# Units of modulation in the opening of a hybrid block kernel: nine of 1, 2, 2, 2, 2, 2, 2, 2 and 1 k tiles in place of eight of two

## The chip, the core and the metric

The kernel runs on one core of one Trainium2 chip. The metric is device time in microseconds. Several executions were timed; the tables give their median. One further execution was profiled, and everything that is said of single instructions comes from it.

The core's engines work side by side and meet through semaphores: TensorE (PE, with its weight loads as PEld), VectorE (DVE), ScalarE (ACT), GpSimd (POOL) and SyncE (SP), which in this kernel issues most of the DMAs. Sixteen DMA engines move the data between HBM and the on-chip memory.

## What is computed

One block with two branches, on 256 tokens of x and 256 tokens of a context, both of width 2048, in f32. Only the start of it matters here:

```python
mod = jax.nn.silu(c) @ w_ada[l] + b_ada[l]
shift, scale, gate = jnp.split(mod[:, None, :], 3, axis=-1)
...
xn = rmsnorm(h, norm_gain[l]) * (1.0 + scale) + shift
cn = rmsnorm(hc, norm_gain[l]) * (1.0 + scale_c) + shift_c
aq, ak, av, ag, hq, hff, hfb, hi, hg, ma, mb = split_columns(xn @ w_in[l])
```

`w_ada` is 2048 x 6144, `w_in` is 2048 x 19456. Columns 0 to 4095 of `mod` (shift and scale) are needed before any normalized column is complete, and each projection sums over all 2048 columns of `xn`. After that come an attention over a window and the context, a gated linear recurrence (HGRN2) in both directions, two output projections, a merge and a last projection.

## The kernel before

**Precision.** A projection operand is split into a high part (`wh`, `xH`), rounded to float32r, and a low part (`wl`, `xL`), the remainder. Three products, high by high, low by high and high by low, are summed in PSUM, so one product of f32 matrices takes three matmuls.

**The opening** (lines 239 to 501) loads x and the context into `X`, transposes them on TensorE (`turn_x`, line 282) so that the model dimension lies on the partitions, and computes the rows' reciprocal roots (`spread_rs`). The 2048 columns are 16 *k tiles* of 128 (`KT` = 16). The list `UNITS` (line 451) cuts them into units `(k, n)`: the first k tile and how many.

For each unit three things happen:

- **Modulation** (`modulation(k, n)`, line 311, a generator). It computes shift and scale for the unit's n x 128 columns, for c and for the context's c at once. In four steps (`k0` = 0, 4, 8, 12) SP loads the unit's columns of `w_ada`, four row tiles at a time, in two DMAs (shift and scale, line 321), into a buffer `raw` of a ring of four; TensorE multiplies them (line 323), four row tiles in four column groups of the array, into the bank `pa`. The bank is copied to `part` (lines 330 and 332), transposed (`tq`, line 336) and reduced on DVE to the columns `mod` (lines 339 to 345). A buffer of the ring always has room for two k tiles, whatever n is.
- **Normalizing** (`modulate(kt)`, line 352), for each k tile of the unit: DVE makes `xm` (line 360), ACT adds the shift and rounds it to `xH` (line 361), DVE takes the remainder `xL` (line 367).
- **First projections** (`first_pieces`, line 407). The opening projects onto 768 columns of `w_in` on the way: 512 of one forget gate and 256 of the other, loaded per unit by `first_loads` (line 389; two DMAs, line 66) and split on ACT and DVE by `first_highs` (lines 400 and 404). Each k tile has 18 matmuls of 512 moving columns (lines 421 and 427), in four pieces of 4, 4, 4 and 6, into six PSUM banks that are held through the whole opening.

**The order** is written out by hand for PE, SP, ACT and DVE (line 460). The first unit's modulation runs first, with fill matmuls into an unused bank in between (`rest`, line 445). Then, for each unit u, its operands are split and normalized, and its pieces run with the modulation of unit u + 1 pushed in between: `plan` (line 476) puts two steps behind piece 0, the other two and the copy to `part` behind piece 2, and the transposes `tq` behind piece 3. Behind piece 3 SP also issues the `w_in` loads of unit u + 1. In a unit of two k tiles the pieces 4 to 7 of its second k tile follow `tq`; they are what TensorE does while DVE and ACT normalize the next unit. SP takes its DMAs in this order, and a load of `w_ada` waits until TensorE has read the ring's buffer four steps before.

After the last unit the six banks are turned to forget gates (`forget`, line 216), and the ordinary projections begin with `proj_tok` (line 745; line 100 is the first of their matmuls). From there only TensorE's order is written out; the order on the other engines comes from priorities and a planner that simulates the engines' times.

Of the kernel before, what the change touches and what calls it, by code (L numbers as in the profile page):

```python
# [17 lines left out]
KT = D // P  # L18
# [20 lines left out]
def block_kernel(ctx: ExitStack, tc: tile.TileContext, x, c, cx, c_ctx, w_ada, b_ada, norm_gain, w_in,  # L39
# [199 lines left out]
    with pl("st", reuse_waits="tile") as st:  # L239
# [65 lines left out]
        def spread_rs():  # L305
            pr_ = ps.tile([P, 512], F32, tag="al2", name="prs")
            pe.matmul(pr_, ones, dgx, start=True, stop=True)
            with tc.high_priority(2 * PRIO):
                act.activation(rsb, pr_, AF.Copy)
# [79 lines left out]
        def first_loads(u, k, n):  # L389

            raws[u] = [wload(w_in, k * P, n, (co,), nc_)[0][:, : n * nc_] for co, nc_ in ((C_FF, 512), (C_FB, 256))]

        def first_highs(u, n):

            tg, nb = FIRST[u % 3]
            f = [wp.tile([P, 1024], F32R, tag=tg_, name=tg_, bufs=3)[:, : n * 512] for tg_ in ("wh", "wl")]
            qt = fp.tile([P, 2, 512], F32R, tag=tg, name="wq", bufs=nb)
            q = [qt[:, r, : n * 256] for r in range(2)]
            for hl, raw in zip((f, q), raws[u]):
                act.activation(hl[0], raw, AF.Copy)  # L400
            fv = [a.rearrange("p (k c) -> p k c", k=n) for a in f]
            chunks[u] = [[a[:, :, :256] for a in fv], [a.rearrange("p (k c) -> p k c", k=n) for a in q],
                         [a[:, :, 256:] for a in fv]]
            return [lambda hl=hl, raw=raw: dve.tensor_tensor(hl[1], raw, hl[0].bitcast(F32), op=ALU.subtract)
                    for hl, raw in zip((f, q), raws[u])]
# [35 lines left out]
        def take(g, n):  # L441
            for _ in range(n):
                next(g, None)
# [4 lines left out]
            for q in range(n):  # L448
                pe.transpose(idle[:, (q % 4) * P: (q % 4 + 1) * P], ident, ident)

        UNITS = [(k, 2) for k in range(0, KT, 2)]
        with tc.manual_schedule(engines={mybir.EngineType.PE, mybir.EngineType.SP}):
            for i in range(4):
                turn_x(i)
# [5 lines left out]
        with tc.manual_schedule(engines={mybir.EngineType.PE, mybir.EngineType.SP, mybir.EngineType.Activation,  # L460
                                         mybir.EngineType.DVE}):
            unit = modulation(*UNITS[0])
            for i in range(4):
                rest(8)
                take(unit, 1)
                if i == 1:
                    spread_rs()
            first_loads(0, *UNITS[0])
            take(unit, 1)
# [6 lines left out]
            plan = {0: 2, 2: 3, 3: 9}  # L476
            for u, (k, n) in enumerate(UNITS):
                lows = first_highs(u, n)
# [3 lines left out]
                after = iter(())  # L482
                if u + 1 < len(UNITS):
                    after = modulation(*UNITS[u + 1])
                if u == 3:
                    bounds()
                for i, _ in enumerate(first_pieces(first, u, k, n)):
                    take(after, plan.get(i, 0))
                    if i == 3 and u + 1 < len(UNITS):
                        first_loads(u + 1, *UNITS[u + 1])  # L490
# [1074 lines left out]
```

## Time and profile before

| | us |
|---|---|
| median of 3 runs | 1593.74 |
| lowest, highest | 1592.25, 1598.02 |
| the profiled execution | 1593.52 |
| its span, from first to last instruction | 1591.7 |
| PE busy in the span | 1567.9 |
| DVE busy | 1182.9 |
| ACT busy | 855.4 |

The profiled execution took 1.8 us more than its span, which is what lies around it. Its time is 0.22 us below the median of the three runs. Busy time counts an engine's instructions; matmuls overlap in the array, and their ends are modelled, so a busy TensorE isn't TensorE at its peak. What counts for it are starts: from one start to the next is what a matmul really takes. Times in the trace are counted from the start of the span. In a row of the timeline stand start, length, engine, line, what is written from what, the tile's form and how many instructions are merged; in brackets the idle time before it and what ended it. A load's "us to landing" runs from its issue on the queue to its completion.

### The profile page before, as it was taken

The numbers are of one execution on the slowest core, as the hardware profiler recorded it, in microseconds if no ns is written. First come the engines' busy times: TensorE is split into PE (matmuls) and PEld (weight loads), VectorE is DVE, ScalarE is ACT, GpSimd is POOL, SyncE is SP. The second block draws the span as 40 slices with busy tenths as digits, with TensorE's granted clock in tenths as the row PEclk, the third lists the DMA queues.
The fourth block names the chain that finished last, engine by engine and source line by source line (L and its number), as shares of the span: only waits on it lengthen the run. The fifth ranks groups of instructions, "written<-read, shape, count | busy, mean of one in ns | idle before, by whom it ended". The sixth has DMA issues, their size and how long they took to land. (4 is left out here: it accounts for less than half of the span.)

```text
span 1591.7 us, 27553 instructions
## 1 busy us (share of the span) xinstructions
PE 1567.9 (99%) x10810; PEld 1341.4 (84%) x10810; DVE 1182.9 (74%) x1745; ACT 855.4 (54%) x1338; POOL 140.5 (9%) x280
## 2 busy tenths in 40 slices
PE   7999999999999999999999999999999999999998
PEld 4567899999888888888888888888887888888887
DVE  4449677777888887787978888887976677757764
ACT  4334443333555555655665566666565776744442
POOL 2000000000000000111121212121112000000000
PEclk9999999999999999999999999999999999999999
DMA  9995533434444444777778777787778854458761
GB/s 369 386 387 174 166 110 131 134 131 133 146 133 136 136 135 130 243 234 230 245 264 271 256 259 244 238 271 240 234 262 262 261 165 149 158 175 288 238 196 70
DMA packets 240851, 333.81 MB, mean 210 GB/s; under 512 B 12080, under 2 KB 157904, under 8 KB 239952
## 3 DMA queue, kind: packets, MB, share of 16 engines
q1 hardware_dynamic: 212048, 249.54, 48.1%
q0 software_dynamic: 19168, 64.08, 11.9%
q10 hardware_dynamic: 9504, 18.42, 3.2%
q8 instruction: 85, 1.39, 0.4%
q14 instruction: 46, 0.38, 0.1%
HBM read 300.53 MB, written 31.47 MB: 209 GB/s over the span
## 5 line engine op out<-in xcount | busy, mean ns | idle before, releaser
L85 ACT ACTIVATE wh<-raw 128x1024 fp32r<-128x1024 f32 x292 | 307.5, 1060 | 257.3 <-PE pj L101 179.1
L86 DVE TENSOR_TENSOR wl<-raw,wh 128x1024 fp32r<-128x1024 f32 x292 | 354.4, 1219 | 122.1 <-ACT wh L85 116.2
L100 PE MATMUL pj<-wh,xHL 128*128 128x512 f32 (+1 forms) x832 | 325.0, 392 | 0.7 <-ACT sg L219 0.7
L101 PE MATMUL pj<-wh,xHL 128*128 128x512 f32 (+1 forms) x832 | 320.3, 386 | 0.0
L103 PE MATMUL pj<-wl,xHL 128*128 128x512 f32 (+1 forms) x832 | 218.5, 386 | 0.0
L100 PEld LDWEIGHTS pj<-wh,xHL 128*128 128x128 f32 x832 | 156.9, 189 | 32.7 <-ACT sg L219 1.9
L101 PEld LDWEIGHTS pj<-wh,xHL 128*128 128x128 f32 x832 | 156.9, 189 | 29.9
L103 PEld LDWEIGHTS pj<-wl,xHL 128*128 128x128 f32 x832 | 154.0, 188 | 31.4
L635 ACT ACTIVATE wh<-T 128x1024 fp32r<-128x1024 f32 x69 | 73.2, 1061 | 149.6 <-DVE T L616 74.0
L635 ACT ACTIVATE wh<-raw 128x1024 fp32r<-128x1024 f32 x92 | 96.9, 1054 | 63.7 <-PE pj L734 23.4
L154 PE MATMUL pj<-xHL,wh 128*128 128x512 f32 x512 | 130.3, 395 | 0.6 <-DVE sgm L1073 0.5
L636 DVE TENSOR_TENSOR wl<-raw,wh 128x1024 fp32r<-128x1024 f32 x92 | 112.0, 1218 | 9.2 <-ACT wh L635 9.1
L154 PEld LDWEIGHTS pj<-xHL,wh 128*128 128x128 f32 x512 | 92.4, 189 | 18.0 <-DVE sgm L1073 0.9
L636 DVE TENSOR_TENSOR wl<-T,wh 128x1024 fp32r<-128x1024 f32 x69 | 84.2, 1220 | 29.7 <-ACT wh L635 29.7
L157 PEld LDWEIGHTS pj<-xHL,wl 128*128 128x128 f32 x512 | 69.9, 190 | 5.8 <-issue 0.7
L157 PE MATMUL pj<-xHL,wl 128*128 128x256 f32 x512 | 71.5, 282 | 0.6 <-issue 0.6
L204 DVE SCALAR_TENSOR_TENSOR acc<-hgw,cg,acc 128x512 f32<-128x512 f32 x60 | 44.8, 747 | 32.7 <-DMA hgw<-in_w_ada_dram 32.7
L918 DVE TENSOR_TENSOR A<-A,X 128x512 f32<-128x512 f32 x96 | 61.7, 684 | 1.6 <-ACT Kmt L848 0.7
L541 POOL DMA_DIRECT2D hgw<-in_w_ada_dram x64 | 34.8, 544 | 273.9 <-DVE acc L204 211.0
L660 PE MATMUL pm<-S,wh 128*128 128x512 f32 x224 | 56.8, 395 | 0.5 <-ACT s L667 0.5
L616 DVE TENSOR_TENSOR T<-raw,T 128x1024 f32<-128x1024 f32 x46 | 56.0, 1218 | 0.0
L616 DVE TENSOR_TENSOR raw<-raw 128x1024 f32<-128x1024 f32 x23 | 28.2, 1225 | 34.9 <-DMA raw<-in_w_in_dram 34.9
(356 smaller groups left out, 3017.9 us busy)
## 6 DMA issues: line engine op xcount, KB each, us to landing
raw<-in_w_in_dram SPq DMA_DIRECT2D x300, 512.0 KB, 4.5
raw<-in_w_ada_dram SPq DMA_DIRECT2D x64, 512.0 KB, 8.0
hgw<-in_w_ada_dram POOLq DMA_DIRECT2D x64, 256.0 KB, 4.4
raw<-in_w_o_hgrn_dram SPq DMA_DIRECT2D x32, 512.0 KB, 3.8
raw<-in_w_o_attn_dram SPq DMA_DIRECT2D x32, 512.0 KB, 4.2
raw<-in_w_out_dram SPq DMA_DIRECT2D x28, 512.0 KB, 3.6
F<-F POOLq DMA_DIRECT2D x16, 512.0 KB, 6.8
F<-F ACTq DMA_DIRECT2D x13, 512.0 KB, 4.4
```

Of the source, the lines that this page charges most:

```text
L85: last_hi[0] = act.activation(h[:, :n], raw[:, :n], AF.Copy).ins
L86: last_lo[0] = dve.tensor_tensor(lo[:, :n], raw[:, :n], h[:, :n].bitcast(F32), op=ALU.subtract).ins
L100: pe.matmul(o, s[0], m[0], start=first, stop=False)
L101: pe.matmul(o, s[1], m[0], start=False, stop=False)
L103: pe.matmul(o, s[0], m[1], start=False, stop=last)
L154: pe.matmul(o.rearrange("p (a t) -> p a t", a=2), h[:, j, cs_], xHL[:, :, k0 + j, :T], start=k0 + j == 0, stop=False)
L157: pe.matmul(o[:, :T], lo[:, j, cs_], xH[:, k0 + j, :T], start=False, stop=k0 + j == KT - 1)
L616: dve.tensor_tensor(o, x_, y_, op=ALU.subtract)
L635: act.activation(h, src, AF.Copy)
L636: dve.tensor_tensor(lo, src, h.bitcast(F32), op=ALU.subtract)
L660: pe.matmul(m_[z].rearrange("p (z a t) -> p z a t", z=2, a=2), h[:, k, :], mv(k), start=fresh and k == 0, stop=False, skip_group_check=True)
L918: dve.tensor_tensor(av, av, f.unsqueeze(3).to_broadcast([P, 2, n2, b]), op=ALU.mult)
```

## The change

One line. `UNITS` was eight units of two k tiles, (0, 2), (2, 2) to (14, 2). Now it is nine: (0, 1), then (1, 2), (3, 2) to (13, 2), then (15, 1).

```diff
-        UNITS = [(k, 2) for k in range(0, KT, 2)]
+        UNITS = [(0, 1)] + [(k, 2) for k in range(1, KT - 1, 2)] + [(KT - 1, 1)]
```

All that takes `(k, n)` follows. With n = 1 a modulation step loads two times 256 KB in rows of 512 B where n = 2 loads two times 512 KB in rows of 1 KB, its matmuls have 256 moving columns instead of 512, `tq` has two transposes instead of four, the unit's `w_in` loads are 256 and 128 KB, and the unit has the pieces 0 to 3 only. `plan` stays as it is, so in unit 0 the transposes of unit 1 stand behind its last piece. The step's buffers and the ring of four stay the same. The code that runs `bounds` with unit 3 now does so one k tile earlier.

## The prediction

> **What bounds the kernel now.** I read the page first, for the stage that the change touches, then the opening in stretches, then the instructions of TensorE and of the DMA queue in it.
>
> ```profile
> span 1591.7 us, 27553 instructions
> PE 1567.9 (99%) x10810; PEld 1341.4 (84%) x10810; DVE 1182.9 (74%) x1745; ACT 855.4 (54%) x1338; POOL 140.5 (9%) x280
> ...
> PE   7999999999999999999999999999999999999998
> ...
> DMA  9995533434444444777778777787778854458761
> ...
> raw<-in_w_ada_dram SPq DMA_DIRECT2D x64, 512.0 KB, 8.0
> raw<-in_w_in_dram SPq DMA_DIRECT2D x300, 512.0 KB, 4.5
> ```
>
> A slice is 39.8 us. TensorE is full from the second slice to the last, so what moves the end of the opening moves the end of the kernel about one to one. The DMA engines are full only in the first three slices. The next view gives stretches of the opening; the columns are PE, PEld, DVE, ACT and POOL busy, then granted clock, DMA share and GB/s.
>
> ```profile
> 0.00:10.00 10.00, 3.57 (x17) 3.57 (x18) 2.76 (x8) 4.07 (x9) 4.30 (x15) 1.00 0.81 309
> 10.00:20.00 10.00, 7.25 (x53) 6.34 (x52) 9.24 (x31) 8.26 (x19) 3.39 (x8) 1.00 1.05 392
> 33.00:40.00 7.00, 5.65 (x39) 2.22 (x41) 2.96 (x7) 0.91 (x2) 0.00 (x0) 1.00 1.08 388
> 86.80:99.60 12.80, 12.80 (x73) 7.81 (x72) 5.61 (x13) 3.85 (x9) 0.00 (x0) 1.00 1.09 386
> 118.20:124.30 6.10, 6.10 (x33) 5.01 (x30) 4.09 (x9) 3.92 (x6) 0.00 (x0) 1.00 0.64 229
> ```
>
> The DMA stream runs at its full 386 to 392 GB/s from 10 us until the last w_ada load, at some 118 us. TensorE is full as well. Its instructions in order of time (start, length) show which of the two is ahead; the last row groups all modulation matmuls to 170 us (busy, mean ns, idle before them):
>
> ```profile
> 20.78 1.06 PE L323 MATMUL pa<-raw,acc 128*32 128x512 f32 x8
> 21.77 1.09 PE L449 MATMUL idle<-cs 128*128 128x128 f32 x8
> 28.74 0.66 PE L449 MATMUL idle<-cs 128*128 128x128 f32 x4
> 32.35 0.73 PE L427 MATMUL pj<-xHL,wh 128*128 128x512 f32 x2
> 37.42 1.07 PE L323 MATMUL pa<-raw,acc 128*32 128x512 f32 x8
> 39.84 1.07 PE L323 MATMUL pa<-raw,acc 128*32 128x512 f32 x8 [1.35 <-DMA raw<-in_w_ada_dram]
> 42.34 0.60 PE L336 MATMUL tq<-cs,part 128*128 128x128 f32 x4
> 42.69 0.71 PE L427 MATMUL pj<-xHL,wh 128*128 128x512 f32 x2
> 46.89 0.62 PE L427 MATMUL pj<-xHL,wh 128*128 128x512 f32 x2
> 51.81 2.03 PE L323 MATMUL pa<-raw,acc 128*32 128x512 f32 x16
> 124.29 0.62 PE L427 MATMUL pj<-xHL,wh 128*128 128x512 f32 x2
> 132.59 0.50 PE L100 MATMUL pj<-wh,xHL 128*128 128x512 f32 x1
> L323 PE MATMUL pa<-raw,acc 128*32 128x512 f32 x256 | 31.8, 601 | 1.4 <-DMA raw<-in_w_ada_dram 1.4
> ```
>
> Call the time from one unit's first projection to the next one's a phase: it holds the unit's 36 projections and the four modulation steps of the unit behind it. Unit 0 starts at 32.35, unit 1 at 46.89, unit 7 at 124.29, and the opening ends at 132.59. Units 1 to 6 take 77.40 us, 12.90 each. A unit's loads are 4.19 MB of w_ada (8 of 512 KB) and 0.79 MB of w_in (512 and 256 KB), 12.87 us at 387 GB/s. So **both are at their limit at once**: the last step of unit 1 waits 1.35 us for its load at 39.84, and 12.87 later, at 52.71, the next one's load is in, where TensorE starts that step at about 52.8 (second half of the x16 row at 51.81).
>
> **The change part by part.** Nine units instead of eight; the first and the last have one k tile. The bytes, the 288 projections and the elementwise work by column stay. There are 8 more w_ada DMAs and 2 more w_in ones on SP, 4 more modulation steps, one more part, tq, red, and so on.
>
> *The first unit comes earlier.* Its four modulation steps have 256 moving columns instead of 512. A step of 512 takes 0.99 us (20.78 to 21.77). No row shows 256. From below, the instructions alone bound it:
>
> ```profile
> 1149.03 1.41 PE al L872 x96
> ```
>
> That is 15 ns for a small matmul, 0.12 us for 8. From above it is 0.99, if the columns aren't what counts. I take half, 0.50, since the 128x512 rows nearest to it run in four column groups at once and leave the weight load little to do. Four steps save 2.0 us, and two of four transposes in tq (0.35 from 42.34 to 42.69) another 0.18. First projection: 32.35 - 2.2 = 30.15. The fill matmuls (idle) stay.
>
> *Its phase loses its cover.* Before, the second k tile's 18 matmuls (42.69 to 46.89, 4.20 us) ran while the next unit's modulation went through DVE and ACT:
>
> ```profile
> 42.97 0.19 DVE L339 TENSOR_REDUCE red<-tq 128x8 f32<-128x32 f32 x1 [6.84 <-PE tq L336]
> 43.60 0.88 DVE L360 SCALAR_TENSOR_TENSOR xm<-X,mod,acc 128x256 f32<-128x256 f32 x2
> 44.12 0.91 ACT L361 ACTIVATE xHL<-xm,mod 128x256 fp32r<-128x256 f32 x2 [1.03 <-DVE xm L360]
> ```
>
> From the end of tq's issue at 42.69 to xH at 45.03 are 2.34 us. Unit 0 has no second k tile, so TensorE now stands for these 2.34 us, once. Behind the waiting matmul stand the modulation steps of unit 2, whose buffers SP waits for. Unit 0's phase: 12.90 - 4.20 + 2.34 = 11.04, and unit 1 starts at 41.19. The 1.35 us wait of 39.84 goes, if unit 1's loads are in by 30.15 + 6.15 = 36.30, the time of its last step (32.35 to 38.5 before, without the wait). They are late next, so:
>
> *The DMA stream runs dry.*
>
> ```profile
> 2.90 15.25 SPq L321 DMA_DIRECT2D raw<-in_w_ada_dram  x8
> 21.90 11.15 SPq L321 DMA_DIRECT2D raw<-in_w_ada_dram  x8
> SPq L321 <- PE pa L323: 12.1, 15, 1.5
> raw<-in_w_in_dram SPq DMA_DIRECT2D x4, 512.0 KB, 3.4
> ```
>
> Unit 1's loads go into unit 0's four buffers, so SP holds them until step 0 has read: 21.90 before, about 21.4 now. Until then only X 4.19, half a unit 2.49, the constants 0.39 and small ones, 7.2 MB, are queued. The windows moved 3.1 MB by 10 us and 7.0 by 20, so it's dry at about 20.7. An undisturbed 512 KB lands in 3.4 us (the last row, stretch 250 to 270 us), 2.1 more than 0.52 MB take at 387 GB/s. Unit 1's 4.19 MB are in at 21.4 + 2.1 + 10.84 = 34.35, before 36.30, so nothing waits. Unit 2's last load is in at 34.35 + 12.87 = 47.2, where TensorE wants it at 41.19 + 5.96 = 47.15. The two are level again, as before. The gap thus costs 0.1; taking landing 1.6 us later, it costs 1.7; below nothing it can't be, as no load comes earlier for it. The ten extra DMAs take SP's issue time, but in unit 0 and unit 8, where SP has less to push.
>
> Rows are 512 B instead of 1 KB in units 0 and 8. Before has both, in the stretches 480 to 500 (512 B) and 250 to 270 us (1 KB); the columns are packets, MB, share of 16 engines:
>
> ```profile
> q1 hardware_dynamic: 4160, 2.10, 35.9%
> q1 hardware_dynamic: 2073, 2.06, 33.2%
> ```
>
> 8% more engine time for the same bytes, 0.4 us a unit. In unit 0 it falls into the dry gap; unit 8's loads are in at 47.2 + 5 x 12.87 + 2.05 + 5.8 = 119.4, where TensorE wants the last one at about 124. Both are hidden; without cover 0.8.
>
> *Units 1 to 8.* Six full phases, 77.40, from 41.19 to 118.59. Unit 7's phase has the half steps of unit 8: 12.90 - 2.0 - 0.18 = 10.72, to 129.31, with its second k tile to hide unit 8's modulation. Unit 8: half of 8.30, 4.15, to 133.46.
>
> **Sum:** 133.46 - 132.59 = +0.87, and 0.1 for the loads: +1 us. The profiled execution took 1593.52 us (span 1591.7), 0.22 below the median of 1593.74; I set the sum on the median. With a step at 0.12 us it is 8 x 0.38 less, -2.0; at 0.99, 8 x 0.49 more, +4.9, and with the late landing +6.5.
>
> TensorE's new stand weighs against the clock too. The granted clock is 1.00 in every stretch quoted, with the 1.35 us wait in one of them.
>
> [...]
>
> **The rivals.**
> - *Only the loads bind, and TensorE's fullness is modelled ends.* Then its 12.90 can shrink to the stream's pace, and the last load sets the end: some 119.4 (121 with the late landing), with behind it a half step 0.5, six matmuls 1.4, tq 0.2, and two k tiles 8.3: 129.8 to 131.4, so -1 to -3, 1590.7 to 1592.7. For it speaks the level race; against it, that the 256 modulation matmuls have 1.4 us of DMA wait in all, this one.
> - *The half step costs a whole one:* +4.9 to +6.5, 1598.6 to 1600.2. For it: no row shows 256 columns.
> - *The ring never fills again, and it ends slower.* Each unit's four buffers were refilled 12.90 us after their release against a landing of 8.0. If the shallower queue at 21 us makes SP wait for TensorE and TensorE for the landing in every phase, each of units 2 to 7 pays the 2.1 us again: +0.9 + 12.6, about 1607. It decides once release to landing exceeds the 12.90. Against it: refills stood at 8.0 under the full stream, and a dry stream lands sooner.
>   [...]
> - *The clock falls in unit 1:* its first k tile takes twice 4.20, +5.1, 1598.8.
> - *The order of ACT and DVE behind the opening comes out otherwise,* as from 133 us only TensorE's is written out and a planner sets the rest. TensorE is busy 1567.9 of 1591.7 us, and 9.2 of its 23.8 idle us lie in the first 20; so at best 14.6 are to be had, 1580, and I take as much for the other sign, 1609.
>
> **How the numbers follow.** Forecast (-1 to +3) 0.63; loads alone 0.12; whole step 0.12; ring 0.04; clock 0.04; order 0.05. The forecast is 1593.74 + 0.9 = 1594.6. The range, 1590.7 to 1600, takes in both bounds of the step and the loads alone. 0.5% is 8 us, about what a measurement tells from no change: faster 0.02, same 0.92, slower 0.06.
>
> **What would show it.** Right: the first projection near 30.2 us, a stand of about 2.3 us before unit 1 ended by ACT's xH, DMA below 387 GB/s for some 2 us after 20 us, no DMA wait at unit 1, phases of 12.9, the opening's end within 2 us of 132.6. Wrong: modulation steps of 256 columns near 0.99 us, DMA waits in most phases, a granted clock under 1.00, or an opening that ends as computed with a kernel that doesn't follow it.

## The result, and the profile after

| | before | after |
|---|---|---|
| median, us | 1592.51 (10 runs) | 1599.97 (10 runs) |
| lowest, highest | 1590.56, 1598.02 | 1595.06, 1605.54 |
| the profiled execution | 1593.52 | 1595.06 |
| its span | 1591.7 | 1593.3 |

The ratio of after to before is 1.0043, with an interval of 1.0026 to 1.0060: 6.8 us longer (4.1 to 9.6). That is inside 0.5%, as forecast, but the forecast was +0.9. The median lies 0.03 us under the range's upper end of 1600. The profiled execution of after is the fastest of its ten, so the 1.5 us by which it is behind the one of before tell too little.

The changed kernel's page, in the lines that answer to those of before:

```profile
span 1593.3 us, 27648 instructions
...
raw<-in_w_ada_dram SPq DMA_DIRECT2D x56, 512.0 KB, 7.9
```

The loads of unit 1 and of those behind it are as large as before, and their median time to landing is the same (7.9 us against 8.0); what differs is when they are issued.

Then TensorE's timeline of the changed kernel, cut to the rows that answer to those of before. Columns are start, length, engine, line, what is written from what, form and count; in brackets the idle time before and what ended it.

```profile
20.31 0.64 PE L323 MATMUL pa<-raw,acc 128*32 128x256 f32 x8
20.88 1.09 PE L449 MATMUL idle<-cs 128*128 128x128 f32 x8
...
29.90 0.72 PE L427 MATMUL pj<-xHL,wh 128*128 128x512 f32 x2
...
38.29 0.60 PE L336 MATMUL tq<-cs,part 128*128 128x128 f32 x4
41.03 1.07 PE L427 MATMUL pj<-xHL,wh 128*128 128x512 f32 x2 [2.15 <-ACT xHL L361]
41.91 1.05 PE L427 MATMUL pf<-xHL,wh 128*128 128x512 f32 x2
42.89 2.77 PE L323 MATMUL pa<-raw,acc 128*32 128x512 f32 x16
45.59 0.73 PE L427 MATMUL pj<-xHL,wl 128*128 128x512 f32 x2
46.16 0.63 PE L427 MATMUL pf<-xHL,wl 128*128 128x512 f32 x2
46.62 1.08 PE L427 MATMUL pj<-xHL,wq 128*128 128x512 f32 x4
47.63 1.93 PE L323 MATMUL pa<-raw,acc 128*32 128x512 f32 x16
...
55.56 0.62 PE L427 MATMUL pj<-xHL,wh 128*128 128x512 f32 x2
...
62.11 1.06 PE L323 MATMUL pa<-raw,acc 128*32 128x512 f32 x8 [0.57 <-DMA raw<-in_w_ada_dram]
...
69.20 0.71 PE L427 MATMUL pj<-xHL,wh 128*128 128x512 f32 x2
...
120.61 0.62 PE L427 MATMUL pj<-xHL,wh 128*128 128x512 f32 x2
...
131.50 0.61 PE L427 MATMUL pj<-xHL,wh 128*128 128x512 f32 x2
...
135.72 0.50 PE L100 MATMUL pj<-wh,xHL 128*128 128x512 f32 x1
```

The first projection is 2.45 us earlier than before (29.90 against 32.35), and the opening's end 3.13 us later (135.72 against 132.59). So 5.6 us were lost in between. The stand of 2.15 us before unit 1, ended by ACT's `xH`, is there. Behind it unit 1 takes 14.53 us (41.03 to 55.56) and unit 2 13.64 (55.56 to 69.20), where a phase was 12.90. Units 3 to 6 are back at 12.85 (69.20 to 120.61, a quarter).

In unit 1 look at the starts: two matmuls of L427 take 0.88 us from 41.03 to 41.91, where two of them at 45.59 and 46.16 take 0.57 and 0.46, and 16 modulation matmuls take 2.70 (42.89 to 45.59) where the next 16 are busy for 1.93. No wait stands there. The view by stretches says why; its columns are PE, PEld, DVE, ACT and POOL busy, the granted clock, the DMA share and GB/s.

```profile
20.00:24.00 4.00, 4.00 (x36) 2.31 (x35) 0.00 (x0) 0.36 (x1) 0.93 (x2) 1.00 0.72 225
24.00:30.00 6.00, 5.58 (x52) 3.86 (x50) 2.37 (x8) 2.24 (x6) 0.00 (x0) 1.00 1.04 349
41.20:44.60 3.40, 3.40 (x12) 1.24 (x16) 3.22 (x8) 0.91 (x2) 0.00 (x0) 0.50 1.09 385
45.00:50.00 5.00, 5.00 (x34) 2.32 (x27) 0.00 (x0) 0.32 (x1) 0.00 (x0) 1.00 1.08 391
```

Two things show. **The clock fell to half** for 3.4 us (0.50 from 41.2 to 44.6), beginning right behind the stand; at half speed these do 1.7 us of work, and unit 1 is 1.63 too long. And **the stream ran dry** as foreseen: 225 and 349 GB/s in the stretches where before had these:

```profile
20.00:24.00 4.00, 4.00 (x33) 1.99 (x32) 0.00 (x0) 0.00 (x0) 1.31 (x3) 1.00 1.09 386
24.00:30.00 6.00, 5.85 (x42) 3.02 (x41) 0.42 (x1) 1.72 (x3) 0.00 (x0) 1.00 1.07 390
```

The load of unit 3's last step is then waited for at 62.11 (0.57 us). Unit 2's last load was issued at 40.25 and took 8.0 us to landing, so it was in at 48.3, against 47.2 in the prediction. TensorE began that step at about 48.5 (second half of the x16 row at 47.63) and didn't wait: at full clock it would have wanted the load at 41.03 + 5.96 = 46.99.

Behind the opening TensorE's order is the one of before, as is GpSimd's. DVE's differs (the sums over tokens against the splits of the weights, up to the copy `vo`), and one wait follows from it, 0.65 us, which before doesn't have:

```profile
181.27 0.47 PE L100 MATMUL pj<-wh,xHL 128*128 128x512 f32 x1 [0.65 <-DVE vo L752]
```

### The profile page after: what moved, and what is told of

Its sections match the earlier page's. It is cut to its first block, busy times and chain, and to the rows that moved or that the text cites. A ratio compares the mean times of both kernels' runs of the same rounds, so it can differ in the third digit from the quotient of the medians.

```text
span 1593.3 us, 27648 instructions
## 1 busy us (share of the span) xinstructions
PE 1568.7 (98%) x10842; PEld 1341.3 (84%) x10842; DVE 1183.5 (74%) x1750; ACT 855.6 (54%) x1341; POOL 140.6 (9%) x280
## 4 chain that ended last, share of the span: by engine, by line
PE 90%; DMA 4%; DVE 3%; issue 2%; ACT 1%; POOL 0%; SPq 0%; POOLq 0%; ACTq 0%; DVEq 0%
PE pj L100 13%; PE pj L101 13%; PE pj L103 13%; PE pj L154 7%; PE pm L660 4%; PE pj L157 4%; PE pj L660 4%; PE pj L737 2%; PE pj L734 2%; PE pj L732 2%; PE pm L663 2%; PE pm L737 2%; PE pm L734 2%; PE pm L732 2%; PE pj L663 2%
## 5 line engine op out<-in xcount | busy, mean ns | idle before, releaser
L86 DVE TENSOR_TENSOR wl<-raw,wh 128x1024 fp32r<-128x1024 f32 x292 | 354.3, 1220 | 119.8 <-ACT wh L85 116.0
L100 PE MATMUL pj<-wh,xHL 128*128 128x512 f32 (+1 forms) x832 | 324.1, 391 | 1.3 <-ACT sg L219 0.7
L100 PEld LDWEIGHTS pj<-wh,xHL 128*128 128x128 f32 x832 | 156.4, 188 | 33.0 <-ACT sg L219 1.9
L636 DVE TENSOR_TENSOR wl<-T,wh 128x1024 fp32r<-128x1024 f32 x69 | 84.2, 1220 | 29.7 <-ACT wh L635 29.7
```

The lines of the kernel that those rows point to most:

```text
L86: last_lo[0] = dve.tensor_tensor(lo[:, :n], raw[:, :n], h[:, :n].bitcast(F32), op=ALU.subtract).ins
L100: pe.matmul(o, s[0], m[0], start=first, stop=False)
L636: dve.tensor_tensor(lo, src, h.bitcast(F32), op=ALU.subtract)
```

## The experiments

The question was which of the two, clock or loads, cost the opening its 2.3 us above the forecast, and whether anything behind the opening adds to it. Each kernel was timed against before on the same chip; the ratio is to that. The opening's end is the start of the first matmul of L100.

| kernel | median | ratio to before (interval) | opening's end |
|---|---|---|---|
| before, four traces | 1592.5 to 1597.5 | 1 | 132.59, 133.23, 132.99, 133.79 |
| after | 1599.97 | 1.0043 (1.0026 to 1.0060) | 135.72 |
| after again (e1) | 1602.20 | 1.0040 (1.0025 to 1.0055) | 136.41 |
| after, third time (e9) | 1602.81 | 1.0031 (1.0015 to 1.0047) | 136.77 |
| fill in the stand (e2) | 1604.01 | 1.0046 (1.0027 to 1.0065) | 139.30 |
| two half units first (e3) | 1604.65 | 1.0049 (1.0027 to 1.0071) | 141.33 |
| two half units last (e4) | 1605.83 | 1.0059 (1.0038 to 1.0081) | 140.22 |
| half steps packed (e5) | 1600.75 | 1.0026 (1.0009 to 1.0042) | 135.72 |
| packed and fill (e6) | 1600.20 | 1.0021 (1.0009 to 1.0033) | 135.84 |
| packed, earlier `tq`, fill (e7) | 1599.71 | 1.0026 (1.0015 to 1.0037) | 134.32 |

**The changed kernel, unaltered, twice more.** Its expectation:

> The changed kernel once more, for a second trace and more times. What has to be explained: the profiled execution of the changed kernel is 1.5 us above that of before, the medians are 7.5 us apart. Clock theory: TensorE's stand of 2.15 us before unit 1 lets the granted clock fall (0.66 in the stretch 41 to 46 us), and how long it stays low differs from execution to execution; then the executions differ in mean granted clock, the slower ones have the lower one, and this trace shows a clock under 1.00 behind 41 us, perhaps for longer than in the first trace. Order theory: the opening costs 3 us as in the first trace and the rest is lost behind 136 us, where VectorE's order to some 180 us differs from that of before; then the clock is no guide and stands of TensorE behind the opening make up over 3 us. Time expected by both: 1597 to 1603.

and for the third time:

> The changed kernel a third time, to set its opening and what lies behind it against traces of the kernel before on one chip. The opening ends 2.5 to 4 us later than in the two traces of before beside it (unit 1's phase 14 to 15 us). Behind it: in the traces with the changed kernel's VectorE order TensorE was 0.5 to 0.6 us late 83 us behind the opening, with the order of before 0. That is expected again, exactly. If all of the median's 6 to 7 us lay in the opening, nothing more would be late at 670 us; the traces so far show 1 to 3 us more there, with a scatter of 1.5.

The opening ends at 136.41 and 136.77, on average of the three traces 136.30, against 133.15 for four of before: +3.15 us, as in the first pair. TensorE stands 2.1 us before unit 1 in both again, the clock falls (the mean from 40 to 60 us is 0.91 in both), and unit 1 takes 14.94 and 15.31. The stretch of e1:

```profile
40.00:60.00 20.00, 18.05 (x94) 9.86 (x95) 10.87 (x25) 5.70 (x11) 0.00 (x0) 0.91 1.09 386
```

Of 20 us 9% are 1.8, so it was half for some 3.5 us. So the fall is no accident of one execution. In the four traces of before it is 1.00 in every stretch from 20 to 60 us.

In both traces TensorE then waits for unit 2's last load, within unit 1. First e1, then e9:

```profile
49.61 1.06 PE L323 MATMUL pa<-raw,acc 128*32 128x512 f32 x8 [0.22 <-DMA raw<-in_w_ada_dram]
```

```profile
50.28 1.07 PE L323 MATMUL pa<-raw,acc 128*32 128x512 f32 x8 [0.56 <-DMA raw<-in_w_ada_dram]
```

Unit 1 starts at 41.73 in e1 and at 42.00 in e9, so at full clock TensorE would have wanted that load 5.96 later, at 47.69 and 47.96. It was in 1.9 and 2.3 us after that. The fall of the clock can't have made it late: it goes into a buffer that TensorE had read in unit 0's phase, before the fall, and from 40 to 60 us the stream stayed full (386 GB/s in both).

**Fill transposes in TensorE's stand.** 18 transposes into the unused bank, behind piece 3 of unit 0, so that the array doesn't stand.

```diff
-                    take(after, plan.get(i, 0))
+                    take(after, plan.get(i, 0)), rest(18 if (u, i) == (0, 3) else 0)
```

> The changed kernel with 18 fill transposes (some 2.2 us of TensorE) behind unit 0's last piece, where it stood for 2.15 us. The order of all other engines is that of the changed kernel. Clock theory: the clock stays at 1.00 from 41 to 46 us, unit 1's phase is back to 12.9 us instead of 14.5, the scatter between executions is that of the kernel before, and the median is 1593.5 to 1595.5 (+1 to +3 us against before). Order theory: the median stays 5 us or more above before. Load theory (half-size loads leave the stream late): a DMA wait of some 1 to 2 us appears in unit 1 or 2 now that unit 1's phase is short, and the opening ends at 134 to 135 us.

TensorE's timeline of this kernel:

```profile
42.42 2.19 PE L449 MATMUL idle<-cs 128*128 128x128 f32 x18 [0.28 <-DVE red L339]
44.36 0.71 PE L427 MATMUL pj<-xHL,wh 128*128 128x512 f32 x2
...
47.48 1.06 PE L323 MATMUL pa<-raw,acc 128*32 128x512 f32 x8 [0.96 <-DMA raw<-in_w_ada_dram]
...
52.81 1.06 PE L323 MATMUL pa<-raw,acc 128*32 128x512 f32 x8 [1.23 <-DMA raw<-in_w_ada_dram]
```

and its stretches, among them one where the clock fell:

```profile
20.20:23.60 3.40, 3.37 (x18) 2.23 (x19) 0.18 (x1) 0.00 (x0) 1.60 (x3) 0.50 0.36 129
42.00:48.00 6.00, 4.76 (x40) 2.94 (x38) 5.54 (x13) 2.10 (x5) 0.00 (x0) 1.00 1.09 383
```

It didn't come out clean. The clock held in unit 1 (1.00), but it had fallen at 20.2 us, in unit 0 and ahead of the place of the edit, which slowed what runs there (the 8 fill transposes before the first step take 1.90 us to the next start, 1.02 in after), so that SP's loads were released later and the stream was emptier (129 GB/s). Up to there the order is that of after, so nothing ties this fall to the edit. With the clock full in unit 1, TensorE now waits for loads there, 0.96 and 1.23 us, and unit 1 takes 15.49. This is the first sign that the two limits cover each other: while the clock is half, TensorE is late enough for little of the loads' delay to be seen as a wait.

**Two half units at the start, all full behind.** The k tiles from 2 on are cut as in before, and the order behind the opening is that of before too.

```diff
-        UNITS = [(0, 1)] + [(k, 2) for k in range(1, KT - 1, 2)] + [(KT - 1, 1)]
+        UNITS = [(0, 1), (1, 1)] + [(k, 2) for k in range(2, KT, 2)]
```

> Units of 1, 1, 2, 2, 2, 2, 2, 2, 2 k tiles: only the front is split, twice, and the last unit is whole. The order of the other engines behind the opening is that of the kernel before. By the steps of the prediction the opening is 3.2 us longer than before (two stands of 2.3, less two half units of modulation). Clock theory: each of two stands lets the clock fall, 1.5 us or more each, so 1597 to 1603 and a wide scatter. Order theory: the order is that of before, so +3 only, 1595 to 1596.5, with a narrow scatter.

TensorE's timeline:

```profile
40.34 0.76 PE L427 MATMUL pj<-xHL,wh 128*128 128x512 f32 x2 [2.12 <-ACT xHL L361]
...
47.81 1.06 PE L323 MATMUL pa<-raw,acc 128*32 128x512 f32 x8 [1.33 <-DMA raw<-in_w_ada_dram]
...
53.04 1.22 PE L427 MATMUL pj<-xHL,wh 128*128 128x512 f32 x2 [2.14 <-ACT xHL L361]
```

Each half unit at the start brings one stand behind it, 2.12 and 2.14 us. The clock fell behind the second alone. The stretches around the second's end and behind the first:

```profile
52.00:56.00 4.00, 2.96 (x12) 1.47 (x16) 3.82 (x9) 1.52 (x4) 0.00 (x0) 0.61 1.08 380
40.00:43.00 3.00, 2.66 (x20) 1.02 (x20) 1.47 (x4) 0.29 (x1) 0.00 (x0) 1.00 1.07 371
```

The mean from 40 to 60 us is 0.91, as with the one fall of e1. Why a stand of 2.12 us passed and one of 2.14 didn't isn't shown. Until 40 us the stream moved 289 GB/s where before had 369 (3.2 MB less, 8.3 us of stream), and the opening ends 8.2 us later. Two half units first are the worse for the loads, as the ring is half empty twice. The expectation had counted two stands and no loads.

**Two half units at the end.** The start is that of before.

```diff
-        UNITS = [(0, 1)] + [(k, 2) for k in range(1, KT - 1, 2)] + [(KT - 1, 1)]
+        UNITS = [(k, 2) for k in range(0, KT - 2, 2)] + [(KT - 2, 1), (KT - 1, 1)]
```

> Units of 2, 2, 2, 2, 2, 2, 2, 1, 1: only the end is split, the first unit is whole. The order behind the opening is that of before but for one VectorE instruction. One stand of 2.3 us, now before the last k tile at some 130 us. By the steps +2.5 us. Clock theory: one fall of the clock there too, so +4 to +8 us, like the changed kernel. Order theory: +2.5 us, 1595. If only a stand near the start, behind the first seconds of the stream, matters, the clock stays at 1.00 here.

TensorE's timeline at the opening's end:

```profile
132.51 0.73 PE L427 MATMUL pj<-xHL,wh 128*128 128x512 f32 x2 [2.27 <-ACT xHL L361]
...
136.62 0.73 PE L421 MATMUL pj<-xHL,wh 128*128 128x512 f32 x2 [2.00 <-DVE xHL L367]
```

Here nearly all of w_ada is in, so the loads can't be what costs at this place. TensorE stands 2.27 us before the last unit and 2.00 within it, until DVE has made `xL`; and from 137.6 to 141.0 the clock is 0.50, which until 140.22 takes another 1.3. That is 5.6 of the opening's +7.1. A half unit at the end without a full one ahead of it thus costs more than one at the start; after's last unit has a full one ahead, and no such stand.

**The ring refilled as before: the half steps packed.** The four half steps of unit 0 are put two into a buffer, so two buffers of the ring stay free, and SP can issue half of unit 1's loads before any step has read.

```diff
-                rv_ = st.tile([P, 2, 4, 256], F32, tag="raw", name="raw", bufs=4)[:, :, :, :w]
+                two_ = st.tile([P, 2, 4, 256], F32, tag="raw", name="raw", bufs=4) if k or k0 % 8 == 0 else two_
+                rv_ = two_[:, :, :, :w] if k else two_[:, k0 // 4 % 2].rearrange("p g c -> p (g c)").rearrange("p (s g c) -> p s g c", s=2, g=4)
```

> The changed kernel, but unit 0's four half steps lie in two buffers of the ring instead of four, so unit 1's first two steps (2.1 MB, 5.4 us of the stream) are loaded without waiting for TensorE. TensorE's order and those of the others behind the opening are the changed kernel's. So far the end of the opening moved with the bytes that the stream lost by 40 us: 2.8, 3.6, 6.0 and 8.3 us of stream lost, opening longer by 3.1, 3.8, 6.7 and 8.7 us (first trace of the change, its repeat, the fill, the front alone). Stream theory (the dry stream is the cause, TensorE's stand and the clock are hidden in it): no dry stretch between 20 and 30 us, no load waits in units 1 and 2, and the median falls to within 3 us of before. Clock theory: the stand of 2.1 us and the clock's fall behind it stay, unit 1's phase stays at 14.5 us, so the opening is still 2.5 to 3 us longer and the median +3 to +6.

Its stretches:

```profile
20.00:24.00 4.00, 3.94 (x34) 2.47 (x35) 0.18 (x2) 0.00 (x0) 1.59 (x3) 1.00 1.09 385
24.00:30.00 6.00, 5.59 (x50) 3.77 (x49) 1.60 (x7) 1.98 (x5) 0.00 (x0) 1.00 1.08 382
42.10:45.50 3.40, 3.40 (x16) 1.24 (x19) 3.22 (x8) 0.91 (x2) 0.00 (x0) 0.50 1.09 386
```

and TensorE's timeline:

```profile
41.80 1.03 PE L427 MATMUL pj<-xHL,wh 128*128 128x512 f32 x2 [2.15 <-ACT xHL L361]
...
56.32 0.62 PE L427 MATMUL pj<-xHL,wh 128*128 128x512 f32 x2
```

This is the clean one. The stream is full from 20 to 30 us (385 and 382), TensorE waits for no load in the whole opening, and unit 1 still takes 14.52, with 3.4 us at half clock: **where no load is missed, the clock alone costs 1.6 us.** Unit 2 is back at 12.87 (56.32 to 69.19), so the 0.74 of after's unit 2 were the loads. The first projection is at 30.68, as in e1 and e9 (30.53 and 30.72; 29.90 in after's first trace), and the opening ends at 135.72, 0.6 before the average of after's three (136.30). That is about what after's three traces waited for loads (0.57, 0.22 and 0.56).

**Packed, with 16 fill transposes in the stand.**

```diff
-                    take(after, plan.get(i, 0))
+                    take(after, plan.get(i, 0)), rest(16 if (u, i) == (0, 3) else 0)
```

> The packed first loads of e5 together with 16 fill transposes in TensorE's stand: neither a dry stream nor a fall of the clock before unit 1. By the steps of the prediction the opening is 0.9 us longer than before, each phase of unit 1 on 12.9 us. Stream and clock theory agree here: +0.5 to +2 us in the median. If the median stays 5 us or more above before, the cause is neither, and lies behind the opening.

TensorE's timeline:

```profile
40.18 1.97 PE L449 MATMUL idle<-cs 128*128 128x128 f32 x16 [0.29 <-DVE red L339]
42.04 0.76 PE L427 MATMUL pj<-xHL,wh 128*128 128x512 f32 x2
...
49.00 1.07 PE L323 MATMUL pa<-raw,acc 128*32 128x512 f32 x8 [0.84 <-DMA raw<-in_w_ada_dram]
...
56.04 0.62 PE L427 MATMUL pj<-xHL,wh 128*128 128x512 f32 x2
```

Its stretches:

```profile
30.00:35.00 5.00, 5.00 (x35) 2.81 (x34) 2.04 (x5) 0.86 (x2) 0.00 (x0) 1.00 1.03 359
35.00:40.00 5.00, 4.89 (x31) 2.46 (x29) 0.07 (x1) 2.01 (x3) 0.00 (x0) 1.00 1.02 339
...
42.00:45.40 3.40, 3.40 (x24) 1.39 (x23) 3.22 (x8) 0.91 (x2) 0.00 (x0) 1.00 1.09 380
```

The transposes kept the clock at 1.00, and unit 1 fell only from 14.52 to 14.00: with TensorE no longer slowed, 0.84 us of waiting for a load came up. The dry stretch has not gone, it has moved to 30 to 40 us (359 and 339 GB/s, where before had 386 and 388), one unit on. Both limits had to be lifted at once, and this version lifted only one of them for good. Its median is 3.4 us above before (1.4 to 5.3), where 0.5 to 2 was expected.

**Packed, unit 1's modulation pulled ahead.** In unit 0 all four steps stand behind piece 0, the copy to `part` behind piece 1 and `tq` behind piece 2, so that piece 3 and 6 transposes cover DVE and ACT.

```diff
-                    take(after, plan.get(i, 0))
+                    take(after, (plan if u else {0: 4, 1: 1, 2: 9}).get(i, 0)), rest(6 if (u, i) == (0, 3) else 0)
```

> The packed first loads, and in unit 0 all four modulation steps of unit 1 behind piece 0, the copy behind piece 1 and the transposes behind piece 2, so that piece 3 (1.4 us) lies beside the normalizing; 6 fill transposes for the rest. The stand of 2.3 us shrinks to about 1. If the loads keep up, the opening is 0.5 us shorter than before: median -1 to +1 us. If loads are late for the four steps in a row (the last is then wanted at some 33.5 us), a load wait of 1 to 2 us appears in unit 0 and the gain is gone.

TensorE's timeline:

```profile
32.07 3.64 PE L323 MATMUL pa<-raw,acc 128*32 128x512 f32 x32
...
40.35 0.73 PE L427 MATMUL pj<-xHL,wh 128*128 128x512 f32 x2
...
47.84 1.07 PE L323 MATMUL pa<-raw,acc 128*32 128x512 f32 x8 [1.41 <-DMA raw<-in_w_ada_dram]
```

Unit 0's phase is 9.41 (30.94 to 40.35) instead of after's 11.13, and the clock holds (1.00 from 40 to 60 us). Unit 1 still takes 14.53, now by 1.41 us of load wait. The opening ends at 134.32, the best of the cuts and 1.2 us behind before. None of these versions is faster than before.

**Before, unaltered, three times more,** for the scatter and for the place of losses behind the opening.

> The kernel before once more, for a trace on this chip: which of the stream's losses and falls of the clock the kernel before has as well. Expected: full stream (over 380 GB/s) from 10 to 118 us, no fall of the clock before 132 us, an opening that ends at 132.6 to 133.5 us.

> The kernel before, a third trace. The opening ends at 132.5 to 133.5 us with a full stream and no fall of the clock in it; the lead of TensorE 83 us behind the opening is that of the other two traces within 0.1 us. TensorE's stand for the loads of the attention queries near 1200 us, 2.5 and 4.8 us so far, comes again, with any length from 0 to 5 us, and with a fall of the clock if it's over 2 us.

> As e10, for the scatter of the kernel before alone: opening 132.5 to 133.5, the stand near 1200 us of any length from 0 to 5 us.

They took 1599.82, 1599.70 and 1598.46 in the one execution each. Set at the same instruction 83 us behind the opening, all seven traces with after's order of DVE (after, e1, e2, e5, e6, e7 and e9) are 0.57 to 0.63 us later than before's, relative to their own opening's end, and e3, with the order of before, is 0.00. At 670 us nothing more is lost than that scatters, and the 0.6 can't be told from it any more: counted from the first trace of before, the four of before lie between 0 and 3.6 us there, the three of after between 0.4 and 2.5. The scatter has a place; in the waits of before's first trace, and of the second one of before, the columns are total, times and longest:

```profile
PE tkt L1104 <- DMA qr<-qr: 2.5, 1, 2.5
```

```profile
PE tkt L1104 <- DMA qr<-qr: 4.8, 1, 4.8
```

Near 1200 us TensorE stands for a DMA for 2.3 to 4.8 us in the four traces of before and 0.5 to 3.3 in the three of after. At the 2.5 us of before's first trace the mean clock is 0.91 (1200 to 1220 us), at the 4.8 us of its second 0.77 (1205 to 1220), and at the 0.5 us of after's first 1.00 (1200 to 1220). The stand is in both kernels. (In e7 TensorE stood 2.2 us at the same line, for DVE, and the mean clock of its span is 0.999; in after, with the one fall in unit 1, it is 0.998.)

## Why the prediction came out as it did

*The first projection earlier: right.* 2.45 us against 2.2; on average of three traces of after and four of before it is 2.1 (30.38 against 32.50). A step of 256 columns takes 0.57 (20.31 to 20.88), near the 0.50 that was taken by half from the step of 512, far from the bounds of 0.12 and 0.99. With it the rival of the whole step falls.

*The phase that loses its cover: right.* Unit 1 starts at 41.03 (41.19 forecast), after a stand of 2.15 (2.34), ended by `xH`.

*The phases further on: right.* Units 3 to 6 take 12.85 (12.90), unit 7 10.89 (10.72), unit 8 4.22 (4.15). The DMA waits don't recur, which refutes the ring that never fills again; loads alone don't bind either, as the phases don't shrink below 12.8.

*The loads: right in kind, and the term of the sum that was mis-sized.* "Unit 2's last load is in at 47.2 where TensorE wants it at 47.15 ... the gap costs 0.1". It was in at 48.3 in the first trace of after, and unit 3's was waited for until 62.11, where a TensorE at full clock would have wanted it at 41.03 + 12.90 + 5.96 = 59.89, 2.2 us before. In e1 and e9 unit 2's was already 1.9 and 2.3 us late by the same measure. In all three traces TensorE waits for a load behind the fall of the clock (0.57, 0.22 and 0.56 us), and that load then sets the time of what follows. So the loads alone account for the 2.3 us above the forecast. That is worked out from these traces. No run shows it by itself: e2, which held the clock in unit 1, had a fall of its own in unit 0.

Two things were left out of the sum. It took the queue for full at once when the first buffer is released, and counted the 2.1 us of one landing alone; the buffers were released one step at a time, and the stretches from 20 to 24 and 24 to 30 us ran at 225 and 349 GB/s. And it put the extra engine time of unit 0's 512 B rows into the gap, although it came ahead of it: from 15 to 18 us the stream ran at 342 to 346 GB/s in the three traces of after and at 376 to 386 in the four of before. (The working's 8% for these rows is 6% when the two rows' bytes, 2.10 and 2.06 MB, are allowed for.) In the first pair the stream lost 27 GB/s on average over the first 40 us (342 against 369), 1.08 MB or 2.8 us.

*The clock: a rival that came true, without a term in the forecast, and covered here by the loads.* The prediction set it at 0.04 and priced it 5.1, on a whole k tile at half speed; the forecast had no term for it. It fell behind the stand of 2.1 to 2.15 us in all three traces of after and in e5. No run shows a whole k tile at half clock: it is 0.50 for 3.4 us (41.2 to 44.6 in after, 42.1 to 45.5 in e5), and costs 1.6 us where no load is late (e5). In the changed kernel itself it adds nothing to the opening's end that the loads don't take anyway. What had been read as evidence was one stretch of before with a wait of 1.35 us and a clock of 1.00, which is shorter. A wait of 1.35 showed nothing of one of 2.15. The trace of before had a nearer case: at its stand of 2.5 us near 1200 us the mean clock is 0.91 (1200 to 1220 us). Nor is the 1.00 of the stretch from 0 to 10 us a reading: the trace of before has no record of the clock ahead of 11.54 us.

*Sum of the opening.* Forecast 133.46 and 0.1 for the loads, measured 135.72. The miss of 2.26 on the working shows as 1.63 in unit 1 and 0.74 in unit 2; all other terms make -0.11 together. The two aren't the costs of two causes to be added: e5 and e6 show that taking one away gives part of the time to the other. The clock alone costs 1.6 (e5); the loads alone cost 1.9 to 2.3 in the changed kernel, and 0.8 to 1.4 are still waited for where the half steps are packed (e6, e7).

*The range: it holds by luck.* Its upper end, 1600, came from a half step that costs a whole one, with the late landing on top. The half step was cheap. What made up the 6.8 us in its place is the forecast's 0.9, the loads' 2.3, some 0.6 behind the opening, and 1 to 3 us that no trace locates.

*The order behind the opening: it did come out otherwise,* but for 0.6 us, not the 14.6 of the bound.

*What stays open.* 3.15 in the opening and 0.6 behind it make 3.75 us, if the 0.6 lasts. The ratios say 6.8 (4.1 to 9.6), 6.4 (4.0 to 8.8) and 4.9 (2.4 to 7.5): the sum lies in the last interval and just below the two others. The 1 to 3 us that remain of the medians could not be located. A profile shows one execution, the first two of after's were the fastest of their series, and the stands near 1200 us move single executions by as much.

## What to carry to other kernels

Where two resources are level, an earlier start is worth nothing until both follow: here 2.45 us were gained on TensorE, and given back with more by a stand and a ring left half empty. Count a ring's depth in bytes in flight, not in buffers, and ask for each piece of work that is removed what it was covering. When an experiment lifts one limit and the time stays, look for the other limit in the same place before dropping the theory.

## What the runs showed of the hardware that was not expected

- The granted clock fell to 0.50 for 3.4 us behind a stand of TensorE of 2.15 us in after (41.2 to 44.6) and in e5 (42.1 to 45.5). In e1 and e9, with a stand of 2.1 us in the same place, its mean from 40 to 60 us is 0.91, as it is in after and e5. Behind the second stand of e3 (2.14 us) it is 0.61 from 52 to 56 us, and behind the second of e4 (2.00 us) 0.50 from 137.6 to 141.0. With fill transposes in the place of the stand before unit 1 it is 1.00 (e2 from 42 to 48 us, e6 from 42.0 to 45.4, e7 from 40 to 60).
- Not every stand of that length brought a fall: behind the first of e3 (2.12 us) the clock is 1.00 from 40 to 43 us, behind the first of e4 (2.27 us) the mean from 132 to 140 us is 0.85, which the half clock from 137.6 accounts for, and e7 with its 2.2 us has a mean of 0.999 over the span. In e2 it was 0.50 from 20.2 to 23.6 us behind stands of 0.62 and 1.14 us, where after has one of 1.14 us and a clock of 1.00 from 20 to 24. What decides between them isn't shown.
- Eight matmuls of 256 moving columns in four column groups took 0.57 us (20.31 to 20.88 in after) where those of 512 took 0.99 (20.78 to 21.77 in before).
- Loads of 256 KB in rows of 512 B ran slower than loads of 512 KB in rows of 1 KB: from 15 to 18 us 342 to 346 GB/s in the three traces of after, 376 to 386 in the four of before, 8 to 11% less. Which of the two, size or row, does it isn't shown.
